# Four sandwich-norm boundaries of a hybrid decoder step: weights split ahead, sums emitted later, two parts of `w_in` by halves, y copied by ScalarE

## The chip, the cores and the metric

One core of a Trainium2 chip runs the whole kernel. The metric is device time in microseconds, the median of repeated executions; the profile is of one further execution. The engines are TensorE (PE, matmuls; PEld its weight loads), VectorE (DVE), ScalarE (ACT), GpSimd (POOL) and SyncE (SP), whose queue issues most DMAs. All of them take their instructions in a fixed order from their own queues and wait for each other by semaphores.

## The reference

One decoder layer over 512 prompt tokens and 8 sequences of 4 new tokens, 544 tokens of width 1024, all in fp32.

```python
def rmsnorm(x, g):
    return x * lax.rsqrt(jnp.mean(x * x, axis=-1, keepdims=True) + EPS) * g

h = h + 0.5 * rmsnorm(swiglu(rmsnorm(h, ffn1_pre_g)), ffn1_post_g)      # FFN 1
u = rmsnorm(h, mix_pre_g)                                               # boundary 1
z, xbc, dt, q, k, v, qi, ki, wi, g_ssd, g_att = split(u @ w_in)
y_ssd = ssd_branch(...)        # Mamba-2 scan
y_att = attend(q, top_k(indexer(qi, ki, wi), 128 or 256), k, v)         # selected keys
merged = sigmoid(g_ssd) * (y_ssd @ w_br_ssd) + sigmoid(g_att) * (y_att @ w_br_att)
h = h + rmsnorm(merged @ w_out, mix_post_g)                             # boundary 2
u = rmsnorm(h, mem_pre_g)
h = h + rmsnorm(mem_attend(u @ w_mq, mem_k, mem_v) @ w_mo, mem_post_g)  # boundary 3
h = h + 0.5 * rmsnorm(swiglu(rmsnorm(h, ffn2_pre_g)), ffn2_post_g)      # FFN 2, end
```

The indexer's scores pick the top keys of each token; the 8 sequences also read old keys and values from paged pools at the picked slots.

## The kernel before

Activations stand transposed, channels on the 128 partitions in 8 column blocks k (or m), tokens along the free axis. The tokens come in half 0 (256 columns) and half 1 (288: 256 prompt, 32 new). Around a norm the work is done by halves, so that one half's norm can run on DVE, ACT and POOL while PE multiplies the other; elsewhere a weight is used on all 544 tokens at once.

Each fp32 operand is split in a high and a low part. `weights()` (L249) loads a weight of up to 2048 columns in two pieces by SP's DMAs into `wr`, ACT copies each to `wh` (L268), DVE subtracts to `wl` (L269; POOL in a few places). There are two `wh`/`wl` buffers, and a cache gives back a weight that is still in one; its test, `wcount - n < WB`, is true of the last one loaded alone. `mm()` (L300) then does three matmuls per k: `wh` by the activation's high part, `wh` by its low part, `wl` by the high part. The result tile is `pg` for all tokens and `pgh` for one half.

A norm of one half is these steps. Squares by ACT are summed over k by POOL (`sq_acc`, L357) into `sqf` for the norm after a block and `sqh` for the norm before the next. `sth` (L402) sums over partitions with a matmul against ones, DVE computes the reciprocal root in a chain of some dozen small instructions on `nw` (L316 to L321), `spread()` scales an identity block by it, `dg` (L421), and a matmul against ones, `pgr` (L422), brings it to all partitions. `bound()` then takes the eight k: y by `pgr` and the gain (L372, DVE), hT + y (L373, DVE for even k, POOL for odd), square and sum of hT, and, where `rt` is given (boundaries 2 and 3), `uh` and `ul` at once (L378, L379), with the second root applied later. At boundary 1 `uh` and `ul` come after a second `sth`, `pgr` pass (L390, L308, L309).

Boundary 1 joins FFN 1's `down_half` (L605) to `first()` in the mixing (L693): parts of `w_in` by halves, c = 0 (indexer key, dt, weights of heads), 1 and 2 (indexer queries `qiT`), 3 (`kT`), half 1 in the reverse order. The four query parts (`C_Q`) come later on all tokens, in `kv()` (L745). Then scores `pid`, top-k on DVE, attention `pqk`, `ppv`, a bisection `pbis`, slot numbers `pslot`, and gathers of cache rows by POOL (L1500) for `pkT`, `psS`, `pO`. Boundary 2 joins `project.out` (L1650, `w_out`) to `queries` (L1711, `w_mq`), boundary 3 `project.out` (`w_mo`) to FFN 2, and the end is `down_half` and the store through `pfo`.

The order is written by `weave` (L103): it runs several generators against a model clock; a generator yields a cost, or a cost and a delay until it is taken up again, such as `yield 0.0, 2.0` ahead of the second norm and `yield 0.1, 3.5` in `spread`. A scheduler of the framework then sets the final order on each engine from that, and it is the same in every execution.

## Time and profile before

| | us |
|---|---|
| median of 3 executions (lowest to highest) | 2295.03 (2291.42 to 2301.48) |
| the profiled execution | 2297.42 |
| its span in the profile | 2295.6 |
| PE busy | 2171.0 |
| DVE busy | 1376.5 |
| ACT busy | 951.2 |
| POOL busy | 470.7 |

The span is what the engines' records cover; the execution's own time has 1.8 us around it. Its mean granted TensorE clock was 0.974 of full speed. Busy time on PE is modelled: matmuls are pipelined, so "busy" does not mean that they come at their best pace, and the pace has to be read from a count of matmuls in a stretch.

In a timeline, the number in square brackets is the engine's idle time ahead of the instruction and what ended it. "x4" joins that many instructions that stand in a row; an fp32 matmul of `sth` or `pgr` shows as two records.

### The profile page before, as it was taken

What the parts mean: (1) busy time and instruction counts of PE and PEld (TensorE: products, weight loads), DVE (VectorE), ACT (ScalarE), POOL (GpSimd) and SP (SyncE); (2) the same over time, 40 slices, a digit from 0 to 9 for tenths busy, and PEclk for the clock granted to TensorE, in tenths of its full rate; (3) what the DMA queues carried; (4) which work ended last, traced back from release to release, by engine and by line L of the source; (5) the groups of instructions that cost most, each with busy time, mean ns of one, the idle gap of its engine ahead of it and who ended that gap; (6) DMA issues with size and microseconds to landing.
All of it is one profiled execution on the core that took longest, in us unless ns stands there. A gap on an engine that the chain in (4) does not pass through costs nothing.

```text
span 2295.6 us, 41583 instructions
## 1 busy us (share of the span) xinstructions
PE 2171.0 (95%) x16751; PEld 2010.4 (88%) x16751; DVE 1376.5 (60%) x2924; ACT 951.2 (41%) x1725; POOL 470.7 (21%) x561
## 2 busy tenths in 40 slices
...
GB/s 191 157 79 138 161 222 150 138 147 232 154 79 97 43 84 89 128 110 144 199 128 132 151 140 154 117 234 112 177 161 132 193 109 157 86 98 89 82 130 104
DMA packets 329757, 311.56 MB, mean 136 GB/s; under 512 B 25625, under 2 KB 301209, under 8 KB 327493
## 3 DMA queue, kind: packets, MB, share of 16 engines
...
## 4 chain that ended last, share of the span: by engine, by line
PE 67%; DVE 15%; issue 5%; POOL 5%; DMA 4%; ACT 4%; SPq 0%; POOLq 0%; DVEq 0%; ACTq 0%
PE pg L300 36%; PE pgh L300 14%; POOL kv L1500 2%; PE pmo L534 2%; DVE wl L269 2%; PE ppv L1070 1%; ACT wh L268 1%; DVE acc L1026 1%; PE pqk L1047 1%; DVE XO L1160 1%; DVE IX L989 1%; DVE m L1025 1%; PE pys L1272 1%; DVE V L988 1%; DVE S L990 1%
## 5 line engine op out<-in xcount | busy, mean ns | idle before, releaser
L268 ACT CAST wh<-wr 128x1024 fp32r<-128x1024 f32 (+2 forms) x382 | 360.9, 960 | 529.6 <-PE pg L300 296.4
L269 DVE TENSOR_TENSOR wl<-wr,wh 128x1024 fp32r<-128x1024 f32 (+2 forms) x358 | 416.0, 1174 | 192.8 <-ACT wh L268 184.3
L300 PE MATMUL pg<-uh,wh 128*128 128x256 f32 (+1 forms) x2336 | 506.2, 296 | 1.6 <-DVE zt L1123 0.9
L300 PE MATMUL pg<-ul,wh 128*128 128x256 f32 (+1 forms) x2336 | 497.4, 293 | 0.8 <-issue 0.8
L300 PE MATMUL pg<-uh,wl 128*128 128x256 f32 (+1 forms) x2336 | 497.5, 293 | 0.0
L300 PEld LDWEIGHTS pg<-uh,wh 128*128 128x128 f32 x2336 | 384.5, 192 | 17.9 <-issue 13.8
L300 PEld LDWEIGHTS pg<-ul,wh 128*128 128x128 f32 x2336 | 383.6, 192 | 7.5 <-issue 6.6
L300 PEld LDWEIGHTS pg<-uh,wl 128*128 128x128 f32 x2336 | 381.8, 191 | 7.9 <-issue 7.1
L300 PE MATMUL pgh<-uh,wl 128*128 128x256 f32 (+1 forms) x880 | 258.1, 296 | 13.4 <-DVE wl L269 13.4
L300 PE MATMUL pgh<-uh,wh 128*128 128x256 f32 (+2 forms) x880 | 260.6, 298 | 3.6 <-ACT uh L308 2.0
L300 PE MATMUL pgh<-ul,wh 128*128 128x256 f32 (+1 forms) x880 | 256.3, 293 | 1.0 <-DVE ul L309 0.6
L300 PEld LDWEIGHTS pgh<-uh,wl 128*128 128x128 f32 x880 | 168.1, 192 | 18.5 <-DVE wl L269 17.1
L300 PEld LDWEIGHTS pgh<-uh,wh 128*128 128x128 f32 (+1 forms) x880 | 169.0, 193 | 7.3 <-ACT uh L308 2.8
L300 PEld LDWEIGHTS pgh<-ul,wh 128*128 128x128 f32 x880 | 169.9, 194 | 3.0 <-DVE ul L309 1.3
L357 POOL TENSOR_TENSOR sqf<-sqf,sqt 128x256 f32<-128x256 f32 (+1 forms) x56 | 61.6, 1100 | 521.3 <-ACT sqt L356 521.2
L300 PE MATMUL pgh<-hh,wh 128*128 128x288 f32 (+1 forms) x352 | 101.8, 289 | 0.0
L300 PE MATMUL pgh<-hl,wh 128*128 128x288 f32 (+1 forms) x352 | 101.2, 288 | 0.0
L300 PE MATMUL pgh<-hh,wl 128*128 128x288 f32 (+1 forms) x352 | 101.0, 287 | 0.0
L1160 DVE SCALAR_TENSOR_TENSOR XO<-CB,convw,XO 128x600 f32<-128x600 f32 x96 | 83.5, 870 | 28.0 <-ACT XO L1158 26.2
...
L269 POOL TENSOR_TENSOR wl<-wr,wh 128x1024 fp32r<-128x1024 f32 x24 | 57.6, 2415 | 133.7 <-ACT wh L268 81.1
L559 DVE TENSOR_TENSOR g<-pg,rt 128x544 f32<-128x544 f32 x32 | 23.2, 725 | 102.8 <-PE pg L300 102.8
...
## 6 DMA issues: line engine op xcount, KB each, us to landing
...
```

The costliest lines, as they stand in the source:

```text
L268: nc.scalar.copy(hi[:, s], r)
L269: (lo_eng or nc.vector).tensor_tensor(lo[:, s], r, hi[:, s].bitcast(F32), op=ALU.subtract)
L300: nc.tensor.matmul(o, a[:, k, c0:c0 + m], x[:, r0:r0 + n], start=(k == 0 and j == 0), stop=(k == KT - 1 and j == 2))
L357: nc.gpsimd.tensor_tensor(acc[:, :n], acc[:, :n], s[:, :n], op=ALU.add)
L534: nc.tensor.matmul(ps[:, :256], a[:, k, i * P:(i + 1) * P], b[:, k, :], start=(k == 0 and j == 0), stop=(k == 7 and j == 2))
L559: nc.vector.tensor_tensor(g1[:, :n], pg, rt[:, sl], op=ALU.mult)
L988: nc.vector.max(v, self.S)
L989: nc.vector.max_index(self.IX[:, r * 8:(r + 1) * 8], v, self.S)
L990: nc.vector.match_replace(self.S, v, self.S, IMM)
L1025: nc.vector.max(m8, acc[:, :W])
L1160: nc.vector.scalar_tensor_tensor(xo, CB[:, j:j + 600], cw(j), xo, op0=ALU.mult, op1=ALU.add)
L1500: nc.gpsimd.indirect_dma_start(out=t[:, hf, :], out_offset=None, in_=(pk, pv)[x], in_offset=off)
```

## The change

The change has seven parts.

- `ahead()` is a new generator: it loads a weight, and ahead of the matmuls that use it also the next one. `down_half`, `first()`, `project.out` and `queries` take their weights from it.
- The cache test is `<=` for `<`: the last two weights are found, which is all that the two buffers hold.
- `sq_acc` gives the last of the eight sums to DVE for `sqf`, and for `sqh` where `rt` is None (boundary 1). Ten sums move.
- Two delays in the model clock are longer: 4.0 for 2.0 ahead of the norm's second `sth`, 4.2 for 3.5 ahead of `dg`.
- `first()` takes six parts by halves, the two new ones the query columns 0 and 1; `kv()` keeps query parts 2 and 3.
- In `project.out` ACT copies y out of PSUM, 32 copies, in place of DVE.
- `dg` has three buffers for two, and the two tiles of `params()` are taken from them in place of a pool of their own.

PE has 15386 instructions before and after: 192 matmuls of all tokens become matmuls by halves. DVE goes from 2744 to 2710, ACT from 1652 to 1672, POOL from 566 to 552, SP's DMAs from 706 to 690.

```diff
--- before.py
+++ after.py
@@ -210,10 +210,7 @@
     def params(self):
 
         nc, I, cp = self.nc, self.I, self.cp
-        ex = ExitStack()
-        lp = self.pool("lp", ex)
-        a = lp.tile([P, P], F32, name="prow")
-        b = lp.tile([P, P], F32, name="prow2")
+        a, b = (self.nw.tile([P, P], F32, tag="dg", name=n, bufs=3) for n in ("prow", "prow2"))
         nc.vector.memset(a, 0.0)
         rows = lambda n: I[n][0].rearrange("(k p) -> k p", p=P)
         for i, n in enumerate(GAINS):
@@ -238,7 +235,6 @@
             nc.vector.tensor_scalar(self.g[n], self.g[n], 0.5, None, op0=ALU.mult)
         nc.scalar.dma_start(self.tri, I["tri"])
         nc.scalar.dma_start(self.caus, I["caus"])
-        ex.close()
 
     def ps1(self, name="ps1"):
         return self.pm.tile([P, 512], F32, tag="pm", name=name)
@@ -249,7 +245,7 @@
     def weights(self, key, parts, KT, lo_eng=None):
 
         nc, wp = self.nc, self.wp
-        if key in self.wcache and self.wcount - self.wcache[key][0] < self.WB:
+        if key in self.wcache and self.wcount - self.wcache[key][0] <= self.WB:
             return self.wcache[key][1]
         W = sum(p.shape[1] for p in parts)
         n = KT * W
@@ -271,6 +267,14 @@
         self.wcache[key] = (self.wcount, (v(hi), v(lo)))
         self.wcount += 1
         return self.wcache[key][1]
+
+    def ahead(self, items, load):
+
+        for n, x in enumerate(items):
+            w = load(x)
+            for nx in items[n + 1:n + 2]:
+                load(nx)
+            yield x, w
 
     def win(self, c0, n=256, lo_eng=None):
         return self.weights(("w_in", c0), [self.I["w_in"][0][:, c0:c0 + n]], 8, lo_eng)
@@ -347,14 +351,14 @@
     def sq_tile(self):
         return self.nw.tile([P, 288], F32, tag="sqt", name="sqt", bufs=2)
 
-    def sq_acc(self, acc, x, n, first):
+    def sq_acc(self, acc, x, n, first, last=False):
         nc = self.nc
         if first:
             nc.scalar.activation(acc[:, :n], x, AF.Square)
         else:
             s = self.sq_tile()
             nc.scalar.activation(s[:, :n], x, AF.Square)
-            nc.gpsimd.tensor_tensor(acc[:, :n], acc[:, :n], s[:, :n], op=ALU.add)
+            (nc.vector if last else nc.gpsimd).tensor_tensor(acc[:, :n], acc[:, :n], s[:, :n], op=ALU.add)
 
     def bound(self, half, sq, post_g, pre_g, rt=None):
 
@@ -372,7 +376,7 @@
                 nc.vector.scalar_tensor_tensor(y[:, k, sl], y[:, k, sl], post_g[:, k:k + 1], r, op0=ALU.mult, op1=ALU.mult)
                 (nc.gpsimd if k % 2 else nc.vector).tensor_tensor(hT[:, k, sl], hT[:, k, sl], y[:, k, sl], op=ALU.add)
             if pre_g is not None:
-                self.sq_acc(acc, hT[:, k, sl], n, k == 0)
+                self.sq_acc(acc, hT[:, k, sl], n, k == 0, last=(k == 7 and rt is None))
             if rt is not None:
                 g = pre_g[:, k:k + 1]
                 nc.scalar.activation(self.uh[:, k, sl], hT[:, k, sl], AF.Copy, scale=g)
@@ -380,7 +384,7 @@
             yield 0.0, 1.0
         if pre_g is None:
             return
-        yield 0.0, 2.0
+        yield 0.0, 4.0
         r = yield from self.rms_h(acc, half)
         if rt is not None:
             nc.scalar.copy(rt[:, sl], r)
@@ -414,10 +418,10 @@
 
         nc = self.nc
         n_all = HALF[half][1]
-        yield 0.1, 3.5
+        yield 0.1, 4.2
         ps = self.ps1("pgr1")
         for i, (c0, n) in enumerate((i * P, min(P, n_all - i * P)) for i in range(-(-n_all // P))):
-            dg = self.nw.tile([P, P], F32, tag="dg", name="dg", bufs=2)
+            dg = self.nw.tile([P, P], F32, tag="dg", name="dg", bufs=3)
             nc.vector.tensor_scalar(dg[:n, :n], self.ident[:n, :n], y[:n, i:i + 1], None, op0=ALU.mult)
             nc.tensor.matmul(ps[:, c0:c0 + n], self.ones[:n, :], dg[:n, :n], start=True, stop=True)
         yield 0.6, 0.5
@@ -605,11 +609,11 @@
         def down_half(hids, half):
             r0, n = HALF[half]
             sl = slice(r0, r0 + n)
-            for m in (range(8) if half == 0 else range(7, -1, -1)):
-                d = self.weights((nm, "d", 1, m), [wd[1408:2816, m * P:(m + 1) * P]], 11)
+            wdm = lambda m: self.weights((nm, "d", 1, m), [wd[1408:2816, m * P:(m + 1) * P]], 11)
+            for m, d in self.ahead(range(8) if half == 0 else range(7, -1, -1), wdm):
                 pd = yield from self.mm(d, hids, 0, half=half)
                 nc.vector.tensor_tensor(y[:, m, sl], pd, y[:, m, sl], op=ALU.add)
-                self.sq_acc(accs[half], y[:, m, sl], n, m == (0 if half == 0 else 7))
+                self.sq_acc(accs[half], y[:, m, sl], n, m == (0 if half == 0 else 7), last=(m == (7 if half == 0 else 0)))
 
         h0, h1 = [], []
         f = Flag()
@@ -686,10 +690,12 @@
         def outs(c):
 
             if c == 0:
-                return wki(), [(0, 104, None)]
-            if c == 3:
-                return self.win(C_K), [(j * P, P, kT[:, j, :]) for j in range(2)]
-            return self.win(C_QI + (c - 1) * 256), [(j * P, P, qiT[:, (c - 1) * 2 + j, :]) for j in range(2)]
+                return [(0, 104, None)]
+            t = kT if c == 3 else qiT[:, (c - 1) * 2:c * 2] if c < 3 else qT[:, (c - 4) * 2:(c - 3) * 2]
+            return [(j * P, P, t[:, j, :]) for j in range(2)]
+
+        def wts(c):
+            return wki() if c == 0 else self.win(C_K if c == 3 else C_QI + (c - 1) * 256 if c < 3 else C_Q + (c - 4) * 256)
 
         f = Flag()
 
@@ -698,9 +704,8 @@
                 if half:
                     yield from f.wait()
                 r0, n = HALF[half]
-                for c in (range(4) if half == 0 else range(3, -1, -1)):
-                    w, ts = outs(c)
-                    for c0, m, t in ts:
+                for c, w in self.ahead(range(6) if half == 0 else range(5, -1, -1), wts):
+                    for c0, m, t in outs(c):
                         ps = yield from self.mm(w, self.xs, c0, m, half)
                         if t is not None:
                             nc.scalar.copy(t[:, r0:r0 + n], ps)
@@ -742,7 +747,7 @@
                 nc.gpsimd.tensor_copy(V[:, :, cols], o.rearrange("p (i c) -> p i c", i=4))
                 nc.gpsimd.tensor_copy(self.vs[:, cols], o2)
                 yield 0.6
-            for c in range(4):
+            for c in (2, 3):
                 w = self.win(C_Q + c * 256, lo_eng=self.nc.gpsimd)
                 for j in range(2):
                     ps = yield from self.mm(w, self.xs, j * P)
@@ -1657,11 +1662,11 @@
             r0, n = HALF[half]
             sl = slice(r0, r0 + n)
             ms = range(8) if half == 0 else range(7, -1, -1)
-            for m in ms:
-                w = self.wcol(name, m // 2)
-                ps = yield from self.mm(w, self.xs, (m % 2) * P, half=half)
-                nc.vector.tensor_copy(y[:, m, sl], ps)
-                self.sq_acc(accs[half], y[:, m, sl], n, m == ms[0])
+            for c, w in self.ahead(range(4) if half == 0 else range(3, -1, -1), lambda c: self.wcol(name, c)):
+                for m in ms[ms.index(2 * c + half):][:2]:
+                    ps = yield from self.mm(w, self.xs, (m % 2) * P, half=half)
+                    nc.scalar.copy(y[:, m, sl], ps)
+                    self.sq_acc(accs[half], y[:, m, sl], n, m == ms[0], last=(m == ms[-1]))
 
         weave(*(side(out(0)) if side is not None else [out(0)]))
         weave(self.bound(0, accs[0], post_g, pre_g, self.rt), out(1), extra=extra)
@@ -1714,12 +1719,13 @@
                 if half:
                     yield from f.wait()
                 r0, n = HALF[half]
-                for m in (range(8) if half == 0 else range(7, -1, -1)):
-                    w = self.wcol("w_mq", m // 2)
-                    ps = yield from self.mm(w, self.xs, (m % 2) * P, half=half)
-                    nc.vector.tensor_tensor(qT[:, m, r0:r0 + n], ps, self.rt[:, r0:r0 + n], op=ALU.mult)
-                    if half:
-                        nc.gpsimd.tensor_copy(own(qz[:, m]), qT[:, m, TP:].rearrange("p (b t) -> p b t", b=8))
+                for c, w in self.ahead(range(4) if half == 0 else range(3, -1, -1), lambda c: self.wcol("w_mq", c)):
+                    for j in ((0, 1) if half == 0 else (1, 0)):
+                        m = c * 2 + j
+                        ps = yield from self.mm(w, self.xs, j * P, half=half)
+                        nc.vector.tensor_tensor(qT[:, m, r0:r0 + n], ps, self.rt[:, r0:r0 + n], op=ALU.mult)
+                        if half:
+                            nc.gpsimd.tensor_copy(own(qz[:, m]), qT[:, m, TP:].rearrange("p (b t) -> p b t", b=8))
 
         def kb_new(b):
             mb = load(I["cache_mem_k"][0, b].rearrange("(i p) h d -> p i (h d)", p=P))
```

PE, boundary 1, half 1, the second norm: `sth` and `pgr` are that norm's matmuls, `pkt` transposes keys of the pool. Before:

```order
3775 L300 MATMUL pgh<-ul,wh 128x256
3776 L300 MATMUL pgh<-uh,wl 128x256
3777 L402 MATMUL sth<-ones,sqh 128x1 x2
3778 L402 MATMUL sth<-ones,sqh 32x1
3779 L422 MATMUL pgr_5636<-dg,ones 128x128 x2
3780 L648 MATMUL pkt<-ident,G 128x128
3781 L422 MATMUL pgr_5636<-dg,ones 128x32
3782 L648 MATMUL pkt<-ident,G 128x128 x15
3783 L300 MATMUL pgh<-uh,wh 128x288 x2
3784 L300 MATMUL pgh<-ul,wh 128x288
```

After:

```order
3819 L304 MATMUL pgh<-ul,wh 128x256
3820 L304 MATMUL pgh<-uh,wl 128x256
3821 L406 MATMUL sth<-ones,sqh 128x1 x2
3822 L406 MATMUL sth<-ones,sqh 32x1
3823 L304 MATMUL pgh<-uh,wh 128x256
3824 L304 MATMUL pgh<-ul,wh 128x256
3825 L304 MATMUL pgh<-uh,wl 128x256
3826 L304 MATMUL pgh<-uh,wh 128x256
3827 L304 MATMUL pgh<-ul,wh 128x256
3828 L304 MATMUL pgh<-uh,wl 128x256
```

Between `sth` and `pgr` there was no other instruction; now 42 weight matmuls stand there (the fence shows the first six), and `pgr` has the numbers 3865 and 3866.

PE, boundary 1, half 0's `pgr` and the sum `sth` of FFN 1's half 1; `hh` and `hl` are the parts of the FFN's hidden activations. Before, `pgr` stood at 3584, 33 weight matmuls ahead of this `sth`, the last rows of which are:

```order
3613 L300 MATMUL pgh<-ul,wh 104x256
3614 L300 MATMUL pgh<-uh,wl 104x256
3615 L300 MATMUL pgh<-uh,wh 128x256
3616 L300 MATMUL pgh<-ul,wh 128x256
3617 L300 MATMUL pgh<-uh,wh 104x256
3618 L402 MATMUL sth<-ones,sqf 128x1 x2
3619 L402 MATMUL sth<-ones,sqf 32x1
3620 L300 MATMUL pgh<-uh,wh 128x256
```

After:

```order
3604 L304 MATMUL pgh<-hh_4386,wh 128x288
3605 L304 MATMUL pgh<-hl_4387,wh 128x288
3606 L304 MATMUL pgh<-hh_4386,wl 128x288
3607 L426 MATMUL pgr_5217<-dg,ones 128x128 x2
3608 L304 MATMUL pgh<-uh,wh 104x256
3609 L304 MATMUL pgh<-uh,wh 128x256
3610 L406 MATMUL sth<-ones,sqf 128x1 x2
3611 L406 MATMUL sth<-ones,sqf 32x1
3612 L304 MATMUL pgh<-uh,wh 128x256
3613 L304 MATMUL pgh<-ul,wh 104x256
```

The last down projections stand directly ahead of `pgr`, and two weight matmuls between it and `sth`.

DVE, boundary 2, half 0, from the `dg` of the norm on; the COPY of y is the copy out of PSUM for half 1, `wl` the split of weights that come next. Before:

```order
1779 L421 TENSOR_SCALAR dg<-ident,nw 128x128 x2
1780 L1663 COPY y<-pgh 128x288
1781 L269 TENSOR_TENSOR wl<-wr,wh 128x1024 x2
1782 L372 SCALAR_TENSOR_TENSOR y<-y,gains,pgr_17582 128x256
1783 L1663 COPY y<-pgh 128x288
1784 L373 TENSOR_TENSOR hT<-hT,y 128x256
1785 L372 SCALAR_TENSOR_TENSOR y<-y,gains,pgr_17582 128x256 x3
1786 L379 SCALAR_TENSOR_TENSOR ul<-hT,gains,uh 128x256 x2
1787 L373 TENSOR_TENSOR hT<-hT,y 128x256
1788 L1663 COPY y<-pgh 128x288
1789 L379 SCALAR_TENSOR_TENSOR ul<-hT,gains,uh 128x256
1790 L372 SCALAR_TENSOR_TENSOR y<-y,gains,pgr_17582 128x256 x2
```

After:

```order
1770 L425 TENSOR_SCALAR dg<-ident,nw 128x128 x2
1771 L265 TENSOR_TENSOR wl<-wr,wh 128x1024 x2
1772 L376 SCALAR_TENSOR_TENSOR y<-y,gains,pgr_17572 128x256 x2
1773 L377 TENSOR_TENSOR hT<-hT,y 128x256
1774 L376 SCALAR_TENSOR_TENSOR y<-y,gains,pgr_17572 128x256 x2
1775 L377 TENSOR_TENSOR hT<-hT,y 128x256
1776 L383 SCALAR_TENSOR_TENSOR ul<-hT,gains,uh 128x256 x3
1777 L376 SCALAR_TENSOR_TENSOR y<-y,gains,pgr_17572 128x256 x2
1778 L265 TENSOR_TENSOR wl<-wr,wh 128x1024 x2
1779 L383 SCALAR_TENSOR_TENSOR ul<-hT,gains,uh 128x256
1780 L377 TENSOR_TENSOR hT<-hT,y 128x256
1781 L383 SCALAR_TENSOR_TENSOR ul<-hT,gains,uh 128x256
```

The copies are gone from DVE, and the third and fourth split stand behind the sixth y; before, they had the numbers 1794 and 1799, behind the seventh.

## Rows read from the trace of the kernel before

**Rows 1.** Page of before, part 1: busy time, share of the span, instructions.

```profile
PE 2171.0 (95%) x16751; PEld 2010.4 (88%) x16751; DVE 1376.5 (60%) x2924; ACT 951.2 (41%) x1725; POOL 470.7 (21%) x561
```

**Rows 2.** PE's waits: engine, line, cause; us in total, times, longest.

```profile
PE pgh L300 <- DVE wl L269: 13.4, 13, 2.0
PE sth L402 <- POOL sqh L357: 12.2, 5, 4.2
PE pgr L422 <- DVE dg L421: 10.4, 5, 3.4
```

**Rows 3.** Windows: us; busy us of PE, PEld, DVE, ACT, POOL; PEclk, DMA.

```profile
455.00:555.00 100.00, 89.87 (x651) 86.36 (x650) 67.76 (x152) 49.26 (x95) 37.61 (x39) 0.95 0.62 178
...
1635.00:1710.00 75.00, 64.67 (x478) 62.52 (x478) 57.92 (x133) 35.17 (x64) 32.52 (x29) 0.95 0.43 136
1829.00:1904.00 75.00, 63.25 (x463) 60.81 (x462) 62.78 (x146) 37.57 (x69) 30.60 (x29) 0.93 0.36 113
2050.00:2100.00 50.00, 50.00 (x402) 50.00 (x402) 16.15 (x18) 14.04 (x19) 0.00 (x0) 1.00 0.34 102
...
521.00:530.00 9.00, 6.26 (x33) 5.79 (x34) 4.63 (x21) 2.62 (x6) 0.22 (x1) 0.62 0.87 259
```

**Rows 4.** Timeline of PE, boundary 1: start, length, instruction, idle time before.

```profile
494.17 0.76 PE L402 MATMUL sth<-ones,sqf 128*128 128x1 f32 x6 [0.98 <-POOL sqf L357]
...
513.42 0.39 PE L300 MATMUL pgh<-uh,wl 128*128 128x256 f32 x1 [1.05 <-DVE wl L269]
...
521.04 0.76 PE L402 MATMUL sth<-ones,sqh 128*128 128x1 f32 x6 [3.31 <-POOL sqh L357]
524.50 1.19 PE L422 MATMUL pgr<-dg,ones 128*128 128x128 f32 x4 [2.70 <-DVE dg L421]
```

**Rows 5.** Timeline of PE, the end of the kernel.

```profile
2277.68 0.76 PE L402 MATMUL sth<-ones,sqf 128*128 128x1 f32 x6 [2.02 <-POOL sqf L357]
2281.14 1.75 PE L422 MATMUL pgr<-dg,ones 128*128 128x128 f32 x6 [2.70 <-DVE dg L421]
```

**Rows 6.** Timeline of PE, boundaries 2 and 3.

```profile
1653.63 0.40 PE L300 MATMUL pgh<-uh,wl 128*128 128x288 f32 x1 [1.62 <-DVE wl L269]
...
1657.45 0.40 PE L300 MATMUL pgh<-uh,wl 128*128 128x288 f32 x1 [1.96 <-DVE wl L269]
...
1698.70 0.76 PE L402 MATMUL sth<-ones,sqh 128*128 128x1 f32 x6 [2.31 <-POOL sqh L357]
...
1847.72 0.40 PE L300 MATMUL pgh<-uh,wl 128*128 128x288 f32 x1 [1.62 <-DVE wl L269]
...
1851.55 0.40 PE L300 MATMUL pgh<-uh,wl 128*128 128x288 f32 x1 [1.97 <-DVE wl L269]
...
1892.59 1.21 PE L402 MATMUL sth<-ones,sqh 128*128 128x1 f32 x6 [4.16 <-POOL sqh L357]
```

**Rows 7.** Instructions of two lines: copies, count, ns min/median/max, starts, forms.

```profile
L1663 DVE COPY y<-pgh x32: 410/434/458, 1613.2 to 1859.2; 128x256 f32<-128x256 f32 x16, 128x288 f32<-128x288 f32 x16
...
L706 ACT COPY qiT<-pgh x8: 348/384/397, 503.9 to 551.0; 128x256 f32<-128x256 f32 x4, 128x288 f32<-128x288 f32 x4
```

**Rows 8.** Timeline of DVE, boundary 1: two splits of 1024 columns.

```profile
505.27 1.23 DVE L269 TENSOR_TENSOR wl<-wr,wh 128x1024 fp32r<-128x1024 f32 x1
...
517.61 1.87 DVE L269 TENSOR_TENSOR wl<-wr,wh 128x1024 fp32r<-128x1024 f32 x1 [0.64 <-ACT wh L268]
```

**Rows 9.** Two tiles: first score matmul and the slots, ns, starts.

```profile
L1014 PE MATMUL pid<-kiT,qiT x48: 376/483/693, 557.2 to 639.2; 64*128 64x256 f32 x16, 64*128 64x384 f32 x16, 64*128 64x512 f32 x16
...
L1461 PE MATMUL pslot<-ident,R x2: 223/233/243, 988.4 to 988.5; 32*128 32x32 f32 x2
```

**Rows 10.** Windows of the selection and gathers; largest wait of DVE.

```profile
644.00:855.00 211.00, 203.79 (x1245) 152.53 (x1242) 185.59 (x410) 111.44 (x268) 41.44 (x29) 0.99 0.25 74
...
994.00:1150.00 156.00, 138.80 (x1044) 115.37 (x1043) 85.96 (x245) 59.29 (x120) 90.02 (x110) 0.89 0.52 155
...
DVE Pm L1048 <- PE pqk L1047: 14.1, 13, 2.3
```

## The prediction

> **What bounds the kernel now.** I read the engine totals first, then TensorE's waits by cause, then the stretches of the four norm boundaries one by one, and last the stretch behind the first of them, because the change moves work into it. TensorE (PE) is busy 2171.0 of 2295.6 us, 95% [rows 1], so an edit pays only where PE stands still or runs slowly. In the list of causes the three largest are those of a norm boundary: 13.4 us for a half weight's low part `wl` from VectorE (DVE), 12.2 us of the column sums `sth` for the last sum from GpSimd (POOL), and 10.4 us of the spread `pgr` for DVE's `dg` [rows 2]. That is 36 us in all, 1.6% of the span, and the list does not count what the clock loses after them.
>
> A quiet stretch gives PE's pace: 402 matmuls in 50.00 us at full granted clock, 8.04 per us or 0.124 us each [rows 3]. By that pace the 651 matmuls of boundary 1 (FFN 1 to mixing) need 81.0 of 100 us, the 478 of boundary 2 (`w_out` to memory) 59.5 of 75, the 463 of boundary 3 (`w_mo` to FFN 2) 57.6 of 75 [rows 3]. So 19.0, 15.5 and 17.4 us are lost in them; this is the most that the change could fetch there. Part of the loss is clock: in the 9 us around boundary 1's longest stalls the granted clock is 0.62 [rows 3]. With levels of 1.2 and 2.4 GHz that is 76% of 9 us, 6.8 us, at the lower one, and half of that, 3.4 us, is lost there.
>
> **Boundary 1, half 1.** Three stalls stand in a row: 1.05 us for `wl`, 3.31 us for the POOL sum, 2.70 us for `dg` [rows 4]. Before, `pgr` follows `sth` on PE with nothing between; in the new order 42 matmuls stand there, 42 x 0.124 = 5.2 us, which covers the 2.70 us. Between half 1's first `pgr` and its second `sth` there are 136 weight matmuls for 95 before, 5.1 us more, which covers the 3.31 us. That filler is the two parts of `w_in` that are now done by halves; their weights are split ahead, so I count the 1.05 us too. Sum 7.06 us, and with the stalls the 3.4 us of clock behind them. Against it stands a new wait: before, 33 matmuls stood between half 0's `pgr` and `sth` of FFN 1's half 1; now two stand there, and the last down-projection matmul comes just before. What `sth` costs straight behind its last matmul is seen at the end of the kernel, 2.02 us [rows 5]; in boundary 1 it is 0.98 us now [rows 4], so I add up to 2.0. Result -3.4 - 7.06 + 2.0 = **-8.5 us**, between -3 (only the 2.70 goes, the rest is renamed) and -12.
>
> **Boundary 2.** Two half-0 matmul groups wait 1.62 and 1.96 us for `wl`, and half 1's sum 2.31 us [rows 6]. The new order has each weight's parts split one column group earlier, in half 1 two `wl` fewer ahead of the last step `y`, and no y copy on DVE. I take these three rows, **-5.9 us**. Bounds: -2 (the split still waits behind DVE's norm steps, since between the y steps of half 0 two `wl` stay) and -12 (nearly all that PE loses beyond the clock's share).
>
> **Boundary 3.** The same two waits, 1.62 and 1.97 us, and 4.16 us for the sum of half 1 [rows 6]. The order here keeps four `wl` ahead of half 1's last `y`, as before, so DVE's chain to the sum is hardly shorter; 7 more matmuls ahead of the sum cover 0.9 us, and 14 more follow between it and its `pgr`. I take the pair and half of the 4.16, **-5.7 us**, between 0 and -12.
>
> **The end.** With three `dg` buffers the third block no longer waits for the first's `pgr`: the six records of `pgr` take 1.75 us where the six of `sth` take 0.76 [rows 5], about **-1.0 us**, between 0 and -1.5. The last sum by DVE saves a part of the 2.02 us ahead of it, inside these bounds.
>
> **Edits at nothing, and their cover.** The 32 y copies go from DVE (434 ns) to ScalarE, ACT (nearest row: 384 ns for the same copy out of PSUM) [rows 7]: 32 x 0.434 = 13.9 us leave DVE, 12.3 us come to ACT. Behind them on ACT are the squares, `wh` and `uh`; ACT is busy 35.17 of 75 us in boundary 2 and 37.57 in boundary 3 [rows 3], so it has room, and the DVE time is already in the terms above. Were ACT late, its `wh` would hold up the `wl`. The cache test that keeps two weights removes reloads at each turn (16 DMAs less on SP's queue, 16 `wh` and 16 `wl`, four of these POOL's): they were issued a weight ahead and hid behind PE's work, except at the boundaries, where I have counted them. The ten sums moved from POOL to DVE cost DVE about 0.45 us each, and DVE's queue is what they may wait in; that is in the lower bounds. The `prow` tiles only matter at the start, where `dg` first comes later; their DMAs on ACT's queue lie far ahead of use, 0, with at most 1 us either way.
>
> The adds and the port: where POOL runs nothing, a `wl` of 1024 columns took 1.23 us, and beside POOL's sums 1.87 for the same [rows 8]. The Trainium skill ("SBUF — State Buffer", Who interferes with whom) says that a VectorE instruction with two SBUF inputs contends with a GpSimd instruction that reads SBUF, by a lock that the first to issue holds for its whole length. The rows agree in sign; by that rule the last sum on DVE would itself be held by a POOL add, and `wl` ahead of the sums would run at its short time. The time it gives is in the first rival.
>
> **The mixing behind boundary 1.** This part goes against the change. The two q parts (192 matmuls) now stand ahead of the indexer. By the new order 3761 weight matmuls precede the first `pid` for 3512 before: 249 x 0.124 = 31 us later, less 8.5, so +22.5 us. The first `pqk` has 3984 ahead in both, the last `ppv` 4752 for 4606 (+146, 18 us), `pslot` 5392 for 5294 (+98, 12 us), the last `pkT` the same 6180. From `pid` at 557.2 to `pslot` at 988.4 it takes 431 us [rows 9]: the selection chain (scores, 32 rounds of top-k on DVE, attention, bisection, slots), then gathers by POOL. If PE's filler sets it, `pslot` comes 22.5 - 18.7 (151 fewer matmuls in between) = +3.7 us. If DVE sets it, +22.5. In its middle DVE is busy 185.59 of 211 us, and PE, busy 203.79, has 1245 matmuls, 155 us by the pace [rows 10]; DVE's largest wait there is for `pqk`, 14.1 us [rows 10], and that is what fewer PE instructions ahead of `pqk` can give back. I take about 7 for that, 4.3 (34 matmuls) for the scores and 4 for the bisection: 22.5 - 15.3, so `pslot` at +7 instead of -8.5. What the gathers' stage does with 15.5 us less lead: it has 1044 matmuls, 130 us, in 156 [rows 10], so it waits already, and its filler shrinks by 98 matmuls. I give back about half of the 15.5: **+7 us**, between 0 and +31 (22.5 and the 8.5).
>
> **Sum.** -8.5 + 7 - 5.9 - 5.7 - 1.0 = -14.1 us. The profiled execution took 2297.42 us, 2.4 over the median of 2295.03 (2291.42 to 2301.48), so 2283.3 on its scale and **2281 us** on the median's. Own range 2274 to 2290, by the middle halves of the bounds.
>
> **Rivals.**
> 1. Everything at the boundaries is kept, and `wl` gets shorter. The mixing absorbs the shift (0 for +7), and at three boundaries four `wl` ahead of POOL's adds take 1.23 for 1.87 us [rows 8], 0.6 x 12 = 7.2. Then -21.1 - 7.2 = -28.3, 2267 us. For it: PE is busy 203.79 of 211 us in the selection [rows 10], so fewer matmuls may shorten it. Against it: the same `wl` still stand between DVE's steps.
> 2. The stalls are renamed. The norm chain itself (steps y, hT, squares, sums, on DVE, POOL and ACT in turn) ends last, and PE waits for `sth` where it waited for `wl`. Left are 2.70 and 3.4 less 2.0 at boundary 1, 1.0 at the end, and the mixing gives back 3: -4.1 - 1.0 + 3 = -2.1, 2293 us. For it: the largest single waits are `sth` after POOL sums, 3.31, 2.31 and 4.16 us [rows 4, 6], and order keeps four `wl` in boundary 3. Against it: 41 and 42 more matmuls stand ahead of boundary 1's second sum and behind it.
> 3. The slower side: DVE paces the selection. `pid` starts 22.5 us later, nothing shrinks, and the gathers wait all of it: +31 on the -8.5, with half of boundaries 2 and 3, -5.8, and -1.0: +15.7, 2311 us. It decides from where `pslot` comes more than 20 us later than 988.4. For it: DVE's 88% there. Against it: the waits of DVE for PE [rows 10].
>
> **How the numbers follow.** Forecast 0.42, kept whole 0.23, renamed 0.22, slower 0.13. The predicted time is the forecast's. The range 2262 to 2302 leaves out most of the slower rival and a little under the first, some 0.15 to 0.2 together. Half a per cent, 11.5 us, is about what a measurement of this kernel can tell from no change: the border of faster is 2283.5. Below it lie 0.26 of the forecast and 0.22 of the first rival, so faster 0.48; within 0.5% the rest of the forecast, the renamed case, and a little of the others, 0.41; slower 0.11.
>
> **What would show it.** Right: in the new trace the `pgr` of boundary 1's half 1 starts without a wait after `sth`, the 0.62 stretch is gone, the waits of `pgh` for `wl` fall from 13.4 to under 6 us, and a new wait of 2 to 3 us stands at `sth` of FFN 1's half 1; `pid` starts near 580, `pslot` near 995. Wrong: `pslot` at 985 or less (first rival) or over 1008 (third); or the waits of `sth` together above 15 us (second).

## The result and the profile after

The changed kernel takes 2314.64 us, median of 7 runs (2307.47 to 2320.03), against 2296.57 us for the kernel before over 7 runs of its own. The ratio is 1.0082, 95% interval 1.0065 to 1.0099: slower, where 0.6% faster was forecast. The profiled execution took 2318.25 us with a span of 2316.3, 20.7 us over that of before.

The page of the changed kernel: the engine totals, the granted clock in 40 slices, and the group of DVE's weight splits.

```profile
PE 2186.1 (94%) x16751; PEld 2022.9 (87%) x16751; DVE 1346.6 (58%) x2890; ACT 946.3 (41%) x1745; POOL 448.9 (19%) x547
...
PEclk9999999999899998997999999999999999999998
...
L265 DVE TENSOR_TENSOR wl<-wr,wh 128x1024 fp32r<-128x1024 f32 (+2 forms) x346 | 398.9, 1166 | 215.6 <-ACT wh L264 211.0
```

The clock in the same slices of the kernel before:

```profile
PEclk9999999999999999979999999999999999999998
```

PE is busy 15 us longer than in [rows 1] with the same number of instructions, and its clock is low in two more slices, the 11th and the 16th (579 to 637 us and 869 to 927). The waits of PE by cause in the changed kernel (us in total, times, longest):

```profile
PE ppt L1069 <- DVE Pm L1063: 11.5, 6, 6.8
PE sth L406 <- POOL sqh L361: 10.7, 3, 3.9
...
PE pkt L652 <- DMA G<-in_cache_kidx,ix: 7.3, 4, 3.8
PE pgr L426 <- DVE dg L425: 6.9, 4, 3.4
PE pgh L304 <- DVE wl L265: 6.7, 7, 2.8
...
PE pid L1019 <- ACT rl L1021: 6.5, 3, 2.8
```

The boundary's three causes of [rows 2] have fallen from 36.0 to 24.3 us, as was meant. Against that stand three causes behind boundary 1: the key transposes `pkt` for their gather G (2.1 us before), the attention's transposes `ppt` for its weights `Pm` (2.3 before) and the scores `pid`, whose PSUM is free once ACT has written `rl` from it (no such wait before).

Where the 21 us came from, from the start times of the same instructions in both traces (first `sth`, last `pgr` of a boundary, first `pid`, `pslot`, last `pO`, and so on):

| stretch | before | after | change | forecast |
|---|---|---|---|---|
| start, FFN 1 | 455.8 | 457.9 | +2.1 | 0 |
| boundary 1, first `sth` to last `pgr` | 68.7 | 71.7 | +3.0 | +1.9 |
| from there to the first `pid` | 32.7 | 60.1 | +27.4 | +20.6 |
| first `pid` to `pslot` | 431.3 | 438.8 | +7.5 | -15.3 |
| `pslot` to the last `pO` | 311.7 | 291.7 | -20.0 | not split |
| rest of the mixing, to boundary 2 | 335.5 | 337.9 | +2.4 | not split |
| boundary 2 and memory | 194.1 | 189.3 | -4.8 | -5.9 |
| boundary 3 and FFN 2 | 412.1 | 415.4 | +3.3 | -5.7 |
| end, to the last `pfo` | 49.0 | 49.1 | +0.1 | -1.0 |

The forecast of +1.9 is the 84 more matmuls that now lie in boundary 1 (10.4 us at the pace) less 8.5; +20.6 is the rest of the 31 us. For the whole way from the first `sth` to boundary 2 the forecast was -1.5, so about -8.7 for the two rows that were not split; measured are, by the unrounded times, +20.5 and -17.5.

Boundary 1 in the changed kernel, timeline of PE, and the same 9 us that had a granted clock of 0.62 in [rows 3]:

```profile
493.96 0.74 PE L406 MATMUL sth<-ones,sqf 128*128 128x1 f32 x6
...
523.81 0.76 PE L406 MATMUL sth<-ones,sqh 128*128 128x1 f32 x6 [1.04 <-DVE sqh L361]
...
529.60 0.61 PE L426 MATMUL pgr<-dg,ones 128*128 128x128 f32 x4
...
521.00:530.00 9.00, 7.96 (x67) 7.72 (x66) 5.23 (x19) 2.67 (x6) 1.79 (x2) 1.00 0.72 248
```

`pgr` after `sth` starts without a wait, the `sth` waits 1.04 in place of 3.31 us [rows 4], the 9 us run at full clock with 67 matmuls for 33, and no new wait stands at 493.96. Then tiles behind the boundary: key transposes, first scores, slots, the last products of the gathered values (median of the durations, first to last start):

```profile
L652 PE MATMUL pkt<-ident,G x128: 270/273/475, 292.4 to 584.4; 128*128 128x128 f32 x128
...
L1019 PE MATMUL pid<-kiT,qiT x48: 375/587/1220, 589.7 to 670.2; 64*128 64x256 f32 x16, 64*128 64x384 f32 x16, 64*128 64x512 f32 x16
...
L1466 PE MATMUL pslot<-ident,R x2: 221/232/244, 1028.6 to 1028.6; 32*128 32x32 f32 x2
...
L1577 PE MATMUL pO<-kv,PZ x256: 272/273/424, 1081.9 to 1320.3; 128*32 128x128 f32 x128
```

```profile
578.06 1.97 PE L652 MATMUL pkt<-ident,G 128*128 128x128 f32 x8 [3.79 <-DMA G<-in_cache_kidx,ix]
...
582.90 1.94 PE L652 MATMUL pkt<-ident,G 128*128 128x128 f32 x8 [1.75 <-DMA G<-in_cache_kidx,ix]
```

The two halves of the last group of key transposes wait for gathers that were issued at 572.5 and 573.8, and the first `pid` follows at 589.7; before, the last `pkt` was at 554.8 and `pid` at 557.2 [rows 9]:

```profile
L648 PE MATMUL pkt<-ident,G x128: 270/272/474, 289.8 to 554.8; 128*128 128x128 f32 x128
```

The stretch from `pid` to `pslot`, before and after, and the gathers after (us; busy us and instructions of PE, PEld, DVE, ACT, POOL; granted clock, DMA share, GB/s):

```profile
557.20:988.50 431.30, 405.53 (x2926) 333.36 (x2926) 362.00 (x933) 209.78 (x454) 89.20 (x106) 0.98 0.34 102
...
589.70:1028.60 438.90, 397.34 (x2775) 322.17 (x2774) 364.60 (x942) 203.85 (x447) 76.48 (x109) 0.93 0.30 90
1028.60:1320.00 291.40, 275.75 (x2180) 234.97 (x2184) 183.68 (x485) 124.33 (x244) 167.42 (x213) 0.92 0.54 160
```

PE has 151 matmuls less to do in it, and yet it is 7.5 us longer, with a granted clock of 0.93 where it was 0.98.

### The profile page after: what moved, and what is told of

It reads as the page before. It is cut to its first block, busy times and chain, and to the rows that moved or that the text cites. A ratio compares the mean times of both kernels' runs of the same rounds, so it can differ in the third digit from the quotient of the medians.

```text
span 2316.3 us, 41480 instructions
## 1 busy us (share of the span) xinstructions
PE 2186.1 (94%) x16751; PEld 2022.9 (87%) x16751; DVE 1346.6 (58%) x2890; ACT 946.3 (41%) x1745; POOL 448.9 (19%) x547
## 4 chain that ended last, share of the span: by engine, by line
PE 68%; DVE 13%; POOL 5%; DMA 5%; issue 5%; ACT 4%; SPq 0%; POOLq 0%; DVEq 0%; ACTq 0%
PE pg L304 37%; PE pgh L304 14%; PE pmo L538 2%; POOL kv L1505 2%; PE ppv L1075 1%; ACT wh L264 1%; DVE wl L265 1%; PE pys L1277 1%; DVE S L995 1%; POOL sqh L361 1%; DVE IX L994 1%; DVE acc L1031 1%; DVE V L993 1%; PE pqk L1052 1%; POOL hT L377 1%
## 5 line engine op out<-in xcount | busy, mean ns | idle before, releaser
L265 DVE TENSOR_TENSOR wl<-wr,wh 128x1024 fp32r<-128x1024 f32 (+2 forms) x346 | 398.9, 1166 | 215.6 <-ACT wh L264 211.0
L304 PE MATMUL pg<-uh,wh 128*128 128x256 f32 x2272 | 493.1, 297 | 7.5 <-ACT CB L1153 6.6
L304 PE MATMUL pg<-uh,wl 128*128 128x256 f32 x2272 | 487.5, 295 | 0.0
L304 PE MATMUL pg<-ul,wh 128*128 128x256 f32 x2272 | 487.0, 295 | 0.0
L304 PE MATMUL pgh<-uh,wh 128*128 128x288 f32 (+3 forms) x944 | 280.6, 299 | 5.5 <-ACT wh L264 2.8
L304 PE MATMUL pgh<-uh,wl 128*128 128x288 f32 (+3 forms) x944 | 278.5, 296 | 6.3 <-DVE wl L265 6.3
L304 PE MATMUL pgh<-ul,wh 128*128 128x256 f32 (+2 forms) x944 | 275.7, 294 | 0.5 <-POOL ul L313 0.5
L304 PEld LDWEIGHTS pgh<-uh,wh 128*128 128x128 f32 (+1 forms) x944 | 182.7, 194 | 9.0 <-ACT wh L264 3.4
L304 PEld LDWEIGHTS pgh<-uh,wl 128*128 128x128 f32 (+1 forms) x944 | 181.4, 193 | 9.4 <-DVE wl L265 8.0
L304 PEld LDWEIGHTS pgh<-ul,wh 128*128 128x128 f32 (+1 forms) x944 | 183.6, 195 | 2.0 <-POOL ul L313 1.1
L566 DVE TENSOR_TENSOR g<-pg,g 128x544 f32<-128x544 f32 x32 | 23.2, 725 | 99.0 <-PE pg L304 99.0
```

Of the source, the lines that this page charges most:

```text
L265: (lo_eng or nc.vector).tensor_tensor(lo[:, s], r, hi[:, s].bitcast(F32), op=ALU.subtract)
L304: nc.tensor.matmul(o, a[:, k, c0:c0 + m], x[:, r0:r0 + n], start=(k == 0 and j == 0), stop=(k == KT - 1 and j == 2))
L566: nc.vector.tensor_tensor(g1[:, :n], pu, g1[:, :n], op=ALU.mult)
```

## Experiments

The theory after the result was the third rival: two query parts put 31 us ahead of the selection, which does not shrink. The rivals: the boundary edits themselves cost the time; or something that happens only with six parts does. The ratios are to the kernel before on the same chip, with 95% intervals. e1 to e4 ran on one chip, e5 to e8b on a second, e9 to e12 on a third, e13 and e14 on a fourth. No kernel but the one before ran on two of them, so that a ratio of one chip holds on another is assumed, not shown.

| kernel | parts | key transposes | boundary edits | ratio |
|---|---|---|---|---|
| changed | 6 | behind | yes | 1.0082 (1.0065 to 1.0099) |
| e1_four | 4 | behind | yes | 0.9989 (0.9970 to 1.0008) |
| e2_six_only | 6 | behind | no | 1.0113 (1.0088 to 1.0137) |
| e3_five | 5 | behind | yes | 0.9986 (0.9970 to 1.0003) |
| e5_q_twice | 6, two of them twice | behind | yes | 1.0110 (1.0082 to 1.0138) |
| e7_keys_first | 6 | ahead | yes | 0.9992 (0.9974 to 1.0009) |
| e14_six_only_keys | 6 | ahead | no | 1.0036 (1.0013 to 1.0059) |
| e13_four_keys_last | 4 | last | no | 1.0035 (1.0015 to 1.0055) |
| e9_before_keys | 4 | ahead | no | 1.0030 (1.0007 to 1.0052) |
| e8b_four_keys_prow | 4 | ahead | yes, but `params()` and `dg` as before | 0.9972 (0.9957 to 0.9986) |

**Which part costs.** In the changed kernel, four parts for six:

```diff
-                for c, w in self.ahead(range(6) if half == 0 else range(5, -1, -1), wts):
+                for c, w in self.ahead(range(4) if half == 0 else range(3, -1, -1), wts):
...
-            for c in (2, 3):          # kv(): query parts on all tokens
+            for c in range(0, 4):
```

> The changed kernel with the two query parts put back behind the first scores: four parts of w_in by halves, everything else of the change stays. Theory 1 (the two parts delay the first score by 31 us of PE work, and the selection chain does not shrink): first pid near 553 to 558, pslot near 990, time 2286 to 2298 us, so at least 15 us under the changed kernel's 2314.6. Rival A (the boundary edits themselves, splits ahead and sums on DVE, cost the time): it stays above 2308 us. Rival B (the boundary gains are whole and only the two parts hid them): 2280 us or less.

Measured: 2293.48 us, `pid` at 557.3, `pslot` at 995.2. The 18 us are gone and the boundary edits are cleared of them; but they also leave next to nothing, so rival B falls too.

The kernel before with six parts, nothing else:

```diff
+            if c > 3:
+                return self.win(C_Q + (c - 4) * 256), [(j * P, P, qT[:, (c - 4) * 2 + j, :]) for j in range(2)]
...
-                for c in (range(4) if half == 0 else range(3, -1, -1)):
+                for c in (range(6) if half == 0 else range(5, -1, -1)):
...
-            for c in range(4):        # kv()
+            for c in (2, 3):
```

> The kernel before with only the two query parts moved: six parts of w_in by halves in first(), none of the other edits. Theory 1: first pid near 590, pslot near 1025, time 2310 to 2322 us. Rival A: within 5 us of the kernel before, 2296.6.

Measured: 2320.69 us, `pid` at 591.7, `pslot` at 1025.5. Six parts alone are enough.

The changed kernel with one query part by halves:

```diff
-                for c, w in self.ahead(range(6) if half == 0 else range(5, -1, -1), wts):
+                for c, w in self.ahead(range(5) if half == 0 else range(4, -1, -1), wts):
...
-            for c in (2, 3):          # kv()
+            for c in range(1, 4):
```

> The changed kernel with one query part by halves instead of two (five parts). The first pid has 96 more weight matmuls ahead of it than in the kernel before, in place of 249. Theory 1, a price per part: 2298 to 2308 us, between the four-part kernel and the changed one, pslot near 1003. If the cost is not of the delay but of something that happens only with six parts (the last key transposes waiting for their gather), it is within 4 us of the four-part kernel.

Measured: 2293.98 us, level with four parts, `pid` at 565.3, `pslot` at 998.5. My price per part missed: one part costs nothing, two cost 20 us. That points to something that only six parts set off.

**What paces the selection.** The last 16 rounds of the sample tokens' top-k left out in the kernel before, the first 128 results copied in their place:

```diff
         for r in range(32):
+            if r == 16:
+                nc.vector.tensor_copy(self.V[:, 128:], self.V[:, :128])
+                nc.vector.tensor_copy(self.IX[:, 128:], self.IX[:, :128])
+            if r >= 16:
+                yield 0.0, 3.6
+                continue
```

> The kernel before, with the last 16 of the 32 top-k rounds of the sample tokens left out and the first 128 results copied in their place: 16 rounds x 3 instructions x 1.21 us, 58 us less on DVE, the same work on PE. If DVE's chain paces the selection: pslot comes 30 to 58 us before 988, and the end 15 to 45 us earlier. If PE's filler paces it: pslot within 8 us of 988, and the end within 8 us of the kernel before.

```profile
560.60:992.80 432.20, 408.46 (x2926) 333.44 (x2926) 306.25 (x855) 209.50 (x454) 87.65 (x106) 0.97 0.34 101
```

Measured: `pid` to `pslot` 432.2 us (431.3 in the kernel before), one run of 2304.04 us. 56 us less on DVE (306.25 for 362.00) change nothing there. The same edit in the changed kernel:

> The changed kernel with 16 of the 32 top-k rounds of the sample tokens left out (58 us less on DVE), as was done to the kernel before, where it left pid to pslot at 432.2 us. If in the changed kernel DVE's queue paces the stretch, it falls from 438.8 to 425 or less, since 151 matmuls have left it. If it stays at 432 to 440, neither TensorE's filler nor DVE's top-k paces it, and the chain of attention and bisection by itself does.

```profile
591.60:1017.80 426.20, 395.23 (x2755) 318.99 (x2754) 307.97 (x858) 201.57 (x444) 76.28 (x103) 0.94 0.32 93
```

Measured: 426.2 us, 12.6 less than in the changed kernel and between the two expectations, one run of 2309.45 us. So with the filler gone DVE paces a part of it, though not all of the 58 us. And the two query parts multiplied once more at their old place, without the copy out of PSUM:

```diff
-            for c in (2, 3):
+            for c in range(4):
                 ...
-                    nc.scalar.copy(qT[:, c * 2 + j, :], ps)
+                    if c > 1:
+                        nc.scalar.copy(qT[:, c * 2 + j, :], ps)
```

> The changed kernel with the two query parts multiplied a second time at their old place, the second result not used: 192 more weight matmuls in the stretch from the first pid to pslot, 23.8 us at the pace of 8.04 per us. If TensorE paces that stretch in the changed kernel, pid to pslot grows from 438.8 by 15 to 24 us and the end comes 12 to 24 us later (2327 to 2339). If it does not (theory 1: there TensorE waits for DVE and ACT and its clock falls), the stretch stays at 430 to 446, the granted clock in it rises over 0.93, and the end is within 8 us of the changed kernel.

```profile
586.00:1031.40 445.40, 413.06 (x2886) 339.07 (x2885) 365.81 (x934) 204.21 (x446) 85.38 (x103) 0.94 0.31 94
```

Measured: 2316.91 us. Of the 192 matmuls only 111 come on top in the stretch (2886 for 2775), since 81 others move behind `pslot`. These 111, 13.8 us at the pace, make it 6.6 us longer, with a clock of 0.94 for 0.93. By the ratios the kernel is 0.28% slower than the changed one, 6 us, with an uncertainty of 0.33%. So PE's filler costs about half of its pace there; it is not free, and neither resource alone sets the stretch.

**The key transposes.** `weave` takes the first generator of its list that is ready; first() is ready nearly always, and `self.side`, the last two groups of key transposes, stands behind it. With four or five parts PE's gap in boundary 1 lets the first of the two groups through at 522 to 532 us; with six the gap is filled and 12 of its 16 instructions come at 568.8. The one buffer G is free only then, the last gather goes out at 572.5, and `pid` stands behind it on PE.

```diff
-        weave(f.after(lead), first(), self.side)
+        weave(f.after(lead), self.side, first())
```

> The changed kernel with the key transposes (pkt) put ahead of first() in the weave, so that six parts no longer push them behind all parts. 3696 weight matmuls ahead of the first pid instead of 3761. Theory 1: the last pkt comes before 570 instead of 584, pid near 575, and most of those 14 us reach the end: 2298 to 2308 us. If the place of the key transposes does not matter, within 5 us of the changed kernel's 2314.6.

Tiles and the selection's window of this kernel:

```profile
L652 PE MATMUL pkt<-ident,G x128: 270/272/421, 291.4 to 528.5; 128*128 128x128 f32 x128
...
L1019 PE MATMUL pid<-kiT,qiT x48: 376/587/1220, 573.5 to 644.4; 64*128 64x256 f32 x16, 64*128 64x384 f32 x16, 64*128 64x512 f32 x16
...
L1466 PE MATMUL pslot<-ident,R x2: 289/298/308, 996.8 to 996.9; 32*128 32x32 f32 x2
...
573.50:996.80 423.30, 397.74 (x2836) 324.26 (x2835) 360.28 (x939) 205.59 (x449) 82.98 (x110) 0.96 0.32 95
```

Measured: 2292.18 us, the whole slowdown back, more than the 14 us expected. The last `pkt` is 56 us earlier than in the changed kernel, `pid` 16, `pslot` 32; the stretch between the two is 15.5 us shorter at a clock of 0.96. `pid` still comes 16 us later than before, and that reaches the end no more.

Is lateness enough without the query parts? The kernel before with the transposes held until first() is done:

```diff
-        weave(f.after(lead), first(), self.side)
+        weave(f.after(lead), chain(first(), self.side))
```

> The kernel before with one edit: the last two groups of key transposes are held until all four parts of first() are done. No query part moves. In its order 3567 weight matmuls precede the first pid for 3512. If the late key transposes are what costs in the changed kernel: pid 12 to 22 us later than in the kernel before, pslot 10 to 25 us later, and the ratio 1.003 to 1.010. If only the moved query parts cost, the ratio is 0.998 to 1.002.

```profile
L648 PE MATMUL pkt<-ident,G x128: 270/272/445, 292.9 to 570.4; 128*128 128x128 f32 x128
...
L1014 PE MATMUL pid<-kiT,qiT x48: 376/587/792, 575.3 to 656.5; 64*128 64x256 f32 x16, 64*128 64x384 f32 x16, 64*128 64x512 f32 x16
```

Measured: ratio 1.0035; the transposes end at 570.4 for 554.8, `pid` comes 18.1 us later, `pslot` at 1017.5, 29 us later where 10 to 25 were expected. `pid` to `pslot` takes 442.2 us, 10.9 more than before with no query part moved. Late transposes cost by themselves: 0.35% for 15.6 us of lateness, where the changed kernel has 29.6 us. And the cure without any boundary edit, the line of e7_keys_first put into e2_six_only:

> The kernel with only the six parts (ratio 1.0113 to the kernel before) with the key transposes put ahead of first(). If the late key transposes cost: ratio 0.998 to 1.004, most of the 1.1% back, without any boundary edit. If the six parts cost by themselves where the boundary edits are absent: 1.008 or more.

Measured: 1.0036, so 0.77 of the 1.13% are back. The same line put into the kernel before, alone:

> The kernel before with only the key transposes put ahead of first() in the weave, no other edit. The four-part kernel with all boundary edits and this order took 2287.0 us. If the boundary edits carry that gain, this one is within 3 us of the kernel before (2293 to 2298). If the order of the key transposes carries it, it is at 2285 to 2290 us, with B1 from its first sth to the first pid as short as there, 97 us.

Measured: 1.0030, slower, on a chip where the kernel before took 2309.2 us, which neither side expected. The transposes ahead are no gain in themselves: with four parts the boundary's gap had room for them. `pid` and `pslot` come 1 us later than before; the trace is longer behind `pslot`, in the stage of the last section, and why stays open.

**A version that beats both.** Four parts, transposes ahead, `params()` and the two `dg` buffers as before, the other edits kept. It is e1_four with the line of e7_keys_first and

```diff
-        a, b = (self.nw.tile([P, P], F32, tag="dg", name=n, bufs=3) for n in ("prow", "prow2"))
+        ex = ExitStack()
+        lp = self.pool("lp", ex)
+        a = lp.tile([P, P], F32, name="prow")
+        b = lp.tile([P, P], F32, name="prow2")
...
-            dg = self.nw.tile([P, P], F32, tag="dg", name="dg", bufs=3)
+            dg = self.nw.tile([P, P], F32, tag="dg", name="dg", bufs=2)
```

> Four parts by halves as before, the key transposes ahead, the parameters' tiles in their own pool and two dg buffers as before; the splits ahead, the cache test, the sums, the delays and y by ACT of the change stay. Theory 1: the start is 2 to 3 us shorter than in the four-part kernel, pid to pslot 430 to 440, time 2286 to 2292 us, 0.1 to 0.4% under the kernel before. Rival (the boundary edits give nothing that lasts): 2293 to 2298 us.

Measured: 2287.02 us for 2293.68, 0.28% under the kernel before and 1.1% under the changed one by the ratios.

**What the pairs say.** Each line compares kernels of the table above that differ in one thing alone (e8b also in `params()` and `dg`); a difference of two ratios is uncertain by 0.2 to 0.35%.

| what differs | pairs | change of the ratio |
|---|---|---|
| two query parts moved, transposes behind | e2 to before, changed to e1 | +1.13%, +0.93% |
| two query parts moved, transposes ahead | e14 to e9, e7 to e8b | +0.06%, +0.20% |
| transposes ahead, six parts | e14 to e2, e7 to changed | -0.77%, -0.90% |
| transposes ahead, four parts | e9 to before, e8b to e1 | +0.30%, -0.17% |
| boundary edits | e1 to before, changed to e2, e7 to e14, e8b to e9 | -0.11%, -0.31%, -0.44%, -0.58% |

The two query parts cost 0.9% and more only while the transposes stand behind them. The end goes with `pslot`: 7 to 10 us late (e1, e7, e3) it costs nothing, 19 and 29 us late (e14, e13) 0.35%, 37 to 43 us late (e2, changed, e5) 0.8 to 1.1%; e9, with 1 us, is the exception. The windows from `pid` to `pslot` of e1, e13, e9, e14 and e8b, in this order, say the same of the selection:

```profile
557.30:995.30 438.00, 415.75 (x2931) 341.60 (x2930) 362.11 (x935) 210.38 (x454) 88.36 (x103) 0.96 0.33 99
...
575.30:1017.50 442.20, 413.60 (x2888) 339.66 (x2887) 363.09 (x934) 205.89 (x449) 85.43 (x103) 0.94 0.32 95
...
558.20:989.60 431.40, 411.65 (x2937) 338.22 (x2936) 361.71 (x933) 206.82 (x451) 88.37 (x105) 0.96 0.34 101
...
580.30:1007.00 426.70, 404.73 (x2835) 330.59 (x2834) 360.57 (x939) 205.57 (x449) 82.76 (x110) 0.94 0.32 94
...
553.90:985.50 431.60, 411.15 (x2937) 338.20 (x2936) 363.71 (x933) 206.72 (x451) 88.46 (x105) 0.96 0.34 100
```

With the transposes ahead, about 100 fewer matmuls (12.6 us at the pace) make it shorter by 4.7 us (e9 to e14) and 8.3 us (e8b to e7): one to two thirds of their pace. With the transposes late that gain is gone: e13, with fewer matmuls than before, takes 442.2 us. e1 takes 438.0 us with all its matmuls and the transposes at 555.0, so the 438.8 of the changed kernel are not the moved parts' doing alone. These are single traces, on four chips.

**The boundary edits one by one**, taken out of that version: y copied by DVE again; no splits ahead in projections and queries; the old delays.

```diff
-                    nc.scalar.copy(y[:, m, sl], ps)                # e10
+                    nc.vector.tensor_copy(y[:, m, sl], ps)
...
-            for c, w in self.ahead(...):                           # e11, the same in queries()
+            for m in ms:
+                w = self.wcol(name, m // 2)
...
-        yield 0.0, 4.0                                             # e12
+        yield 0.0, 2.0
...
-        yield 0.1, 4.2
+        yield 0.1, 3.5
```

> The four-part kernel with the key transposes ahead (2287.0 us), with y of the two projections copied by DVE again instead of ACT. In it boundary 3 takes 75.5 us and boundary 2 67.4 from the first sth to the last pgr. If ACT's copies are what made ACT's weight copies late there, boundary 3 falls by 2 to 4 us. If DVE's time was the limit, both grow by 2 to 6 us. The total moves by less than 0.3% either way.

> The same base (2287.0 us) without the splits ahead in the projections and the queries; FFN 1 and first() keep them. If the splits ahead are what boundary 2 gained, its 67.4 us go back to 69 to 71, and the waits of pgh for wl come back in boundaries 2 and 3 (5 us more). If the norm chain (steps, sums, sth) ends last anyway, boundaries 2 and 3 stay within 1.5 us of 67.4 and 75.5 and only the names of the waits change.

> The same base (2287.0 us) with the two delays of the model clock as before (2.0 and 3.5). If the later place of the sums is what covers the sth and pgr stalls, waits for sth and dg grow by 5 us or more in all and boundary 1 from its first sth to its last pgr takes 2 us more than 70.2. If the delays only rename stalls, all three boundaries stay within 2 us.

Measured: ratios 0.9988 (0.9969 to 1.0006), 0.9953 (0.9930 to 0.9976) and 0.9963 (0.9941 to 0.9984), around the base's 0.9972. Boundary 2 took 67.6, 65.8 and 64.4 us for 67.4 in the base, boundary 3 75.8, 78.9 and 71.4 for 75.5. With the stretches behind them (memory, FFN 2), which take up what is moved, the pairs are 190.3, 190.1, 189.8 for 191.0 and 412.6, 414.9, 411.4 for 412.3. None of these three edits is worth more than 3 us there, and the longer delays are worth nothing that shows. The cache test, the sums on DVE and the splits ahead in FFN 1 and first(), which stay in all three, were not taken out. On the same chip e9, with the transposes ahead and no edit, took 2316.83 us and these three 2304.47, 2297.37 and 2301.61, so the edits together are worth 12 to 19 us there, each difference uncertain by some 7 us; which of them carries that stays open. PE's waits in the base (first) and without the splits ahead (second):

```profile
PE sth L410 <- POOL sqh L365: 11.1, 3, 4.2
PE pgr L430 <- DVE dg L429: 8.4, 5, 3.4
PE pgh L308 <- DVE wl L269: 7.4, 10, 2.5
```

```profile
PE pgh L308 <- DVE wl L269: 11.3, 13, 2.8
PE pgr L430 <- DVE dg L429: 8.0, 4, 3.4
PE sth L410 <- POOL sqh L365: 6.0, 3, 2.8
```

Without the splits ahead `wl` is waited for 3.9 us more and the sums 5.1 us less: the stall changes its name. Neither expectation held in full, with boundary 2 shorter by 1.6 us and boundary 3 longer by 3.4.

## Why the prediction was wrong

**The step that failed** is the one on the mixing, +7 us, in two of its terms: the 31 us of delay ahead of `pid`, and the 15.3 us that the selection was to give back.

I read the 249 matmuls ahead of `pid` as the delay of the two query parts, though these are 192. The other 57 were the sign: they had moved ahead because the key transposes had moved back. With the transposes ahead, e7's order has 3696 ahead of `pid` for 3761; with the transposes alone held back, e13's has 3567 for 3512. I followed the parts past PE's queue and never asked who stands behind first() in the list, or where the gather for the last group is issued. `pid` came 32.5 us late for 22.5, and what that costs is the transposes' doing: -0.77% and -0.90% with them put ahead, while the two query parts beside them cost 0.06% and 0.20%, 1 to 5 us, which is not clear of nothing. From e8b to e7 `pid` comes 19.6 us later and `pslot` 11.3, much as I had added up for the parts alone; but the edit did more.

**"What fewer PE instructions can give back"** was too much, and its source was wrong. I took 15.3 us out of the selection for 151 fewer matmuls, 18.7 us; it became 7.5 us longer, and `pslot` came 40 us late for 7. About 7 of the 15.3 were to come out of DVE's wait for `pqk`, 14.1 us [rows 10]. In the changed kernel, from 589 to 894 us (`pid` to the last `ppv`), it is

```profile
DVE Pm L1053 <- PE pqk L1052: 18.8, 19, 2.2
```

and in the same stretch of e2 and e7, also with fewer matmuls, 14.1 and 15.8 us: nothing came out of it. Where such matmuls were moved alone (e5, e9 to e14, e8b to e7) they were worth one to two thirds of their pace, not 15.3 of 18.7. The late transposes took even that back: e13 is 10.9 us longer with none of the parts moved. How they do it is not shown; the waits for `Pm` and `rl` and the granted clock of 0.93 for 0.98 are what the trace has in that place. The rows behind `pslot` gave back 17.5 us, twice the forecast; how much of that is their 98 fewer matmuls was not tried apart.

The third rival had `pslot` over 1008 and 2311 us, near the 1028.6 and 2314.64. It was right in sign, but not in mechanism: it let DVE pace the selection, and 56 us less on DVE changed nothing before (e4) and 12.6 us after (e6); it put the whole price on the query parts, and e7, with the same parts ahead, is level with the kernel before. It also let the whole delay reach the end, where 17.5 us of it did not. That its time came so near is luck.

**Boundary 1 was right**: forecast +1.9 with the filler, measured +3.0; the stalls of 1.05 and 2.70 us and the low clock went as said, that of 3.31 us fell to 1.04. The new wait at FFN 1's `sth` did not come; a 1.01 us wait for `uh` did, just ahead of it.

**Boundaries 2 and 3 were too large**: forecast -11.6, measured -1.5 with their neighbours. Both are in the main the second rival: the stalls were renamed. Boundary 2's -4.8 is near its term of -5.9, but not by its mechanism. No wait for `wl` is left there, where the kernel before has 1.62, 1.96, 2.00 and 0.82 us; but the sum of half 1, which was to lose its 2.31 us, waits 3.85, and that of half 0 waits 3.00 for 0.46. The rows of the kernel before that [rows 6] does not have, three of boundary 2 and one of boundary 3:

```profile
1663.42 0.61 PE L402 MATMUL sth<-ones,sqh 128*128 128x1 f32 x4 [0.46 <-POOL sqh L357]
...
1689.97 0.38 PE L300 MATMUL pgh<-uh,wl 128*128 128x256 f32 x1 [2.00 <-DVE wl L269]
...
1693.78 0.38 PE L300 MATMUL pgh<-uh,wl 128*128 128x256 f32 x1 [0.82 <-DVE wl L269]
...
1857.51 0.61 PE L402 MATMUL sth<-ones,sqh 128*128 128x1 f32 x4 [2.00 <-POOL sqh L357]
```

Rows of boundary 2, of boundary 3 and of the end in the changed kernel:

```profile
1684.58 0.61 PE L406 MATMUL sth<-ones,sqh 128*128 128x1 f32 x4 [3.00 <-POOL sqh L361]
...
1719.34 0.79 PE L406 MATMUL sth<-ones,sqh 128*128 128x1 f32 x6 [3.85 <-POOL sqh L361]
...
1873.89 1.01 PE L406 MATMUL sth<-ones,sqh 128*128 128x1 f32 x4 [3.87 <-POOL sqh L361]
...
1909.50 0.39 PE L304 MATMUL pgh<-uh,wh 128*128 128x256 f32 x1 [2.78 <-ACT wh L264]
...
1912.77 0.58 PE L304 MATMUL pgh<-uh,wl 128*128 128x256 f32 x1 [2.77 <-DVE wl L265]
...
2298.48 0.73 PE L406 MATMUL sth<-ones,sqf 128*128 128x1 f32 x6 [1.74 <-DVE sqf L361]
2301.91 1.75 PE L426 MATMUL pgr<-dg,ones 128*128 128x128 f32 x6 [2.70 <-DVE dg L425]
```

In boundary 3, in place of the pair of 1.62 and 1.97 and the 4.16 us [rows 6] stand 3.87 for the sum of half 0 (2.00 before), and 2.78 and 2.77 for `wh` and `wl` of half 1. That the splits ahead take their time from the engines of the norm's chain fits e11, where the sums waited 5.1 us less without them, but boundary 3 was no shorter there: it is argued, not shown. The sign that I had named for this rival, waits of `sth` over 15 us together, could not tell: they are 13.4 us now (10.7, 1.7 and 1.0) and were 15.2 before (12.2 and 3.0). And the waits for `wl` fell to 6.7 us, not under 6.

The first rival's shorter splits came at boundary 1 alone. The mean of the 1024-column splits there went from 1523 to 1337 ns, at boundary 2 from 1393 to 1365, at boundary 3 from 1327 to 1362, where the rival had 1230. Over the whole kernel the mean is 1166 ns in the changed kernel's page above and 1174, with other lengths mixed in, in that of before:

```profile
L269 DVE TENSOR_TENSOR wl<-wr,wh 128x1024 fp32r<-128x1024 f32 (+2 forms) x358 | 416.0, 1174 | 192.8 <-ACT wh L268 184.3
```

The Trainium skill ("SBUF — State Buffer", Who interferes with whom) says that a VectorE instruction with two SBUF inputs, as such a split is, contends with a GpSimd instruction that reads SBUF. No run here took the adds away, so the means show only how long the splits took, not how often the two met.

**The end**: the 1.0 us was a misreading. With three buffers the six `pgr` records still take 1.75 us behind a wait of 2.70, as in [rows 5]; their length was not the wait for the third `dg`. **The start**: forecast 0 with at most 1 us, measured about 2, of which one wait shows that the kernel before does not have:

```profile
51.26 0.30 PE L223 MATMUL ps_par<-ident,prow 128*128 128x128 f32 x1 [1.66 <-DMA prow<-in_ffn_post_g]
```

`prow`, whose tile now comes from the `dg` buffers, waits there for its DMA; that the buffers are why is argued. The six kernels that keep the change's `params()` take 182.7 to 185.1 us to the first `pmo`, a matmul that stands beside FFN 1, the others 181.0 to 183.2, so all that can be said is 1 to 2 us.

**The range** ended at 2302 and left most of the third rival out. Its chance of 0.13 was too low for a change that put `pid` off by 31 us of PE work, 57 matmuls of it without a reason that I had found.
